# Encoder trunk on one core: x loaded once and transposed on TensorE, TensorE in the order of the source

## The chip, the core and the metric

The kernel runs on one core of a Trainium2 chip. A core has five engines, each with its own queue of instructions: TensorE (PE: products and transposes), VectorE (DVE), ScalarE (ACT), GpSimd (POOL) and SyncE (SP, which here only starts transfers), and 16 DMA engines. PE reads from SBUF and writes to PSUM, which holds eight banks here, four under the tag "g" and four under "y". The metric is the device time of one execution in microseconds; lower is better.

## The reference

Two layers over x of 256 positions by 1024 (float32). Cut to what matters:

```python
for l in range(2):
    h_res = h_res + 0.5 * swiglu(rmsnorm(h_res, ffn1_norm[l]), ffn1_w_gate[l], ffn1_w_up[l], ffn1_w_down[l])
    z = rmsnorm(h_res, mix_norm[l]) @ w_in[l]
    zq, zk, zv, zp, hq, hi, hff, hfb, hg = jnp.split(z, split_idx, axis=-1)
    y_att = dilated_attention(zq, zk, zv, q_norm[l], k_norm[l], biases)
    y_pool = pool_mixer(zp, pool_w[l], pool_scale[l])
    y_rec = hgrn2_bidirectional(hq, hi, hff, hfb, hg, lb_all[0, l], lb_all[1, l], hgrn_norm[l])
    h_res = h_res + jnp.concatenate([y_att, y_pool, y_rec], axis=-1) @ w_out[l]
    h_res = h_res + 0.5 * swiglu(rmsnorm(h_res, ffn2_norm[l]), ffn2_w_gate[l], ffn2_w_up[l], ffn2_w_down[l])
```

`swiglu` is `(silu(h @ w_gate) * (h @ w_up)) @ w_down` with a width of 2816. The recurrence (`hgrn2`) is a gated linear attention in both directions, with 4 heads of 64 each.

## The kernel before

x stays in SBUF as `self.x` (two tiles of 128 positions by 1024). The weights of all six stages (feed-forward, mixer, feed-forward, twice) stream through SBUF as 329 "halves" of 128x1024 float32 (512 KB), on SP's queue, through four buffers (`stage`). Each half is split into `whi` (rounded, by ACT, line 149) and `wlo` (the remainder, line 151, by DVE, or by POOL where the list `POOL_HALVES` names the half). Each product is made of three: hi by hi, hi by lo, lo by hi (lines 167 to 169 with 256 columns, lines 174 to 176 with 512). A half feeds 12 products of 512 columns or 24 of 256. The splits run `LOOK` = 4 halves ahead of the products, in five buffers.

*Feed-forward stage.* Eleven blocks of 256 of the width: `gate_up` makes gate and up of a block from four halves (48 products, `gu`), silu and product give `h`, `turn` transposes it (`hp`), and `down` adds the block of before to `ya`, from two halves. `ya` has four quarters, named by (dh, tt): 512 columns dh of the 128 positions tt.

*From stage to stage.* In the last `down` of a stage, each quarter is done after 6 products. Then `add` puts it on x (DVE, line 371), `squares` sums its squares for the norm (ACT, line 283), and `turn` transposes the four 128x128 blocks of the quarter (PE, `xps`, line 296); after both tt of a dh, `parts` splits the result into `xh` (ACT, line 274) and `xl` (DVE, line 275), the operands of the next stage. For quarter (1,1) the transposes are `pending`: `late_turn` runs them inside the next stage's first products. At the end of a mixer it is the same with `wo` in place of `ya`.

*Mixer.* After the gates, the steps of the string `ORDER` run: `c:n` makes the products of half n of the input projection (2 halves of hq, 4 each of q, k and zh, 2 of hg, 4 of v); `mm:m`, `up:m`, `put:m` are the levels of the recurrence (products `lev`, line 541, operands U and W updated by DVE in line 520, results put into A); `ns`, `nq`, `nk` scale and transpose q and k (`zq`, `tp`, line 660); `sc`, `tr`, `pv` are the attention; `rec` the product of the recurrence and `rnorm` its norm; `o` the output projection (`wo`).

*What sets the order.* SP issues in the order of the source. On the other engines a scheduler sets the order by its own estimates, within the dependencies, PE's queue too: a product can come ahead of transposes that stand before it in the source. Each engine then runs its queue in that order, and waits for what its next instruction needs.

*The start.* x comes in twice: in blocks already transposed (`x_t`, four transfers into the buffer of the later `bias`) between the two pieces of the first half on SP's queue, and as it is, on ACT's queue.

Of the kernel before, what the change touches and what calls it, by code (L numbers as in the profile page):

```python
# [16 lines left out]
P = 128  # L17
# [36 lines left out]
    ),  # L54
    (
# [8 lines left out]
T2 = 10  # L64
# [6 lines left out]
class Trunk:  # L71
    def __init__(self, ctx, tc, x_in, xt_in, wall, prm_in, rel_in, cst_in, cst2_in, msk_in, band_in, y_out):
# [18 lines left out]
        self.pending = None  # L91
# [11 lines left out]

        self.xt0 = self.bias[:, 0]
        self.cp.tile([P, 16], F32, name="pad0")
        xr = xt_in.rearrange("p (k t) -> p k t", k=KC)
# [3 lines left out]
        for j in range(4):  # L110
            if j < 2:
                q = slice(j * HALF // 2, (j + 1) * HALF // 2)
                nc.sync.dma_start(w0[:, q], wall[0][:, q])
            nc.sync.dma_start(self.xt0[:, 2 * j:2 * j + 2, :], xr[:, 2 * j:2 * j + 2, :])
        self.feed_dma(2)
        self.prm_in, self.cst_in = prm_in, cst_in
        self.ident = self.cst[:, K_ID:K_ID + P]
        nc.scalar.dma_start(self.ident, cst_in[:, K_ID:K_ID + P])
        nc.scalar.dma_start(self.x, x_in.rearrange("p (t d) -> p t d", t=2))
# [38 lines left out]
    def ahead(self, i):  # L158

        self.feed_dma(i + LOOK + 4)  # L160
        self.feed_split(i + LOOK)
# [21 lines left out]
    def late_turn(self):  # L183

        if self.pending is not None:
            self.pending()
            self.pending = None

    def gate_up(self, i0, gu, mid=None):

        for q in range(4):
            if q == 1:
                self.late_turn()
            if q == 2 and mid is not None:
                mid()
            self.ahead(i0 + q)
            wh, wl = self.half(i0 + q, 2)
            for tt in range(2):
                s = slice(tt * P, tt * P + P)
                for kk in range(2):  # L200
                    k = 2 * q + kk
                    self.mm3t(gu[tt], self.xh[:, k, s], self.xl[:, k, s], wh[:, kk, :], wl[:, kk, :],
                              start=(k == 0), stop=(k == KC - 1))
# [118 lines left out]
    def ffn(self, stage, post):  # L322
# [11 lines left out]
        for b in range(NB):  # L334
            if b == min(4, NB - 1) and stage == 0:
                self.setup(silu)
# [53 lines left out]
    def setup(self, after):  # L390
# [3 lines left out]
        mskf = self.mx.tile([P, 2 * len(LEVELS), 64], F32, tag="Kp", name="mskf", bufs=2)  # L394
        with self.tc.issue_after(after.ins):
            nc.scalar.dma_start(cst2, self.cst2_in)
            nc.scalar.dma_start(rel, self.rel_in)
            nc.scalar.dma_start(self.cst[:, K_BO:], self.cst_in[:, K_BO:])
            nc.scalar.dma_start(self.prm[:, C_PW:], self.prm_in[:, C_PW:])
            nc.scalar.dma_start(mskf, self.msk_in.rearrange("p (l c) -> p l c", c=64))  # L400
            nc.scalar.dma_start(self.band, self.band_in.rearrange("p (g s t) -> p g s t", g=4, s=2))
        nc.vector.tensor_copy(self.msk, mskf)
# [46 lines left out]
    def mixer(self, l):  # L449
# [106 lines left out]
        def lev_put(m):  # L556
# [20 lines left out]
            else:  # L577
                V["Ao"] = tl("Kp", [P, 8, P], bufs=2)
# [22 lines left out]
        def head_rs(sq, tag):  # L601
# [3 lines left out]
            hi, lo = self.split(sq)  # L605
# [176 lines left out]
        def out(nm):  # L782
# [14 lines left out]
            "rnorm": rec_norm, "o": out,  # L797
# [6 lines left out]
    def body(self):  # L804
        nc = self.nc
        self.new_xt()
        for j in range(4):
            if j < 2:
                self.split_part(0, j * HALF // 2, (j + 1) * HALF // 2)
            for k in (2 * j, 2 * j + 1):  # L810
                self.parts(0, k, self.xt0[:, k, :])
        self.n_split = 1
        self.feed_split(2)
        for dh in range(2):
            for tt in range(2):
                self.squares(0, dh, tt)
# [49 lines left out]
def _pack(inp):  # L866
# [40 lines left out]
    xt = np.ascontiguousarray(inp["x"][0].T.reshape(KC, P, T).transpose(1, 0, 2).reshape(P, KC * T))  # L907
    return x, xt, wall, prm
# [44 lines left out]
```

## Time and profile before

| | us |
|---|---|
| median of 3 runs (lowest to highest) | 1042.7 (1040.74 to 1046.78) |
| profiled execution, its own time | 1040.81 |
| its span, from first to last instruction | 1039.0 |
| PE busy | 1004.4 |
| DVE busy | 585.0 |
| ACT busy | 538.8 |
| POOL busy | 88.3 |
| mean granted clock of PE | 0.993 |

The span is what the trace shows; the execution's own time is 1.8 longer than it. A granted clock of 1.00 is 2.4 GHz and 0.50 is 1.2 GHz; the mean tells how much of the time PE ran at the higher level.

### The profile page before, as it was taken

How to read it: one execution, taken by the hardware profiler on the slowest of the kernel's cores; microseconds unless marked ns; L12 is line 12 of the kernel's file. 1: busy time of each engine (PE TensorE's matmuls, PEld its weight loads, DVE VectorE, ACT ScalarE, POOL GpSimd, SP SyncE). 2: the span in 40 equal slices, each digit the busy share in tenths (PEclk: the TensorE clock that was granted, in tenths of full speed). 3: DMA queues.
4: the chain of work that ended last, by engine and by line, in shares of the span. 5: the costliest groups of instructions: out<-in, count | busy, mean ns of one | idle time of the engine just before them, and what ended most of it. 6: DMA issues, size and time to landing. Idle time of an engine off the chain costs nothing.

```text
span 1039.0 us, 14421 instructions
## 1 busy us (share of the span) xinstructions
PE 1004.4 (97%) x5682; PEld 826.2 (80%) x5682; DVE 585.0 (56%) x776; ACT 538.8 (52%) x774; POOL 88.3 (8%) x43
## 2 busy tenths in 40 slices
PE   6999999998999999999999999999889999999998
PEld 4878888886867888888878888889768678888886
DVE  5655555669835555555565555554977155555553
ACT  7544444684865544444564444447648555444442
POOL 0000000140230000000000000004132400000000
PEclk9999999999999999999999999999989999999999
DMA  7769655553334555555555555554523346555551
GB/s 265 245 219 329 234 188 193 165 163 123 103 122 136 179 192 182 186 192 188 185 168 187 190 185 186 195 185 138 165 83 102 102 147 196 184 185 189 194 186 58
DMA packets 50420, 182.20 MB, mean 175 GB/s; under 512 B 5768, under 2 KB 6024, under 8 KB 49968
## 3 DMA queue, kind: packets, MB, share of 16 engines
q1 hardware_dynamic: 48528, 174.09, 51.6%
q0 software_dynamic: 720, 4.21, 1.1%
q10 hardware_dynamic: 1104, 2.99, 0.8%
q8 instruction: 44, 0.72, 0.3%
q14 instruction: 24, 0.20, 0.1%
HBM read 180.20 MB, written 3.16 MB: 176 GB/s over the span
## 4 chain that ended last, share of the span: by engine, by line
PE 87%; DVE 6%; ACT 3%; issue 3%; DMA 1%; POOL 0%; SPq 0%; ACTq 0%; DVEq 0%; POOLq 0%
PE gu L175 15%; PE gu L176 15%; PE gu L174 15%; PE ya L174 8%; PE ya L176 8%; PE ya L175 8%; PE hp L352 2%; PE wo L174 2%; PE wo L175 1%; PE wo L176 1%; ACT whi L149 1%; DVE wlo L151 1%; PE xps L296 1%; DMA bias<-x_t 1%; PE lev L541 1%
## 5 line engine op out<-in xcount | busy, mean ns | idle before, releaser
L149 ACT ACTIVATE whi<-stage 128x1024 fp32r<-128x1024 f32 (+1 forms) x329 | 347.1, 1056 | 395.3 <-PE gu L176 202.3
L151 DVE TENSOR_TENSOR wlo<-stage,whi 128x1024 fp32r<-128x1024 f32 (+1 forms) x294 | 360.7, 1229 | 337.5 <-ACT whi L149 337.4
L174 PE MATMUL gu<-whi,xh 128*128 128x512 f32 x704 | 275.7, 392 | 8.0 <-ACT xh L274 5.7
L175 PE MATMUL gu<-wlo,xh 128*128 128x512 f32 x704 | 274.9, 391 | 0.5 <-DVE wlo L151 0.5
L176 PE MATMUL gu<-whi,xl 128*128 128x512 f32 x704 | 274.7, 390 | 0.0
L174 PEld LDWEIGHTS gu<-whi,xh 128*128 128x128 f32 x704 | 132.5, 188 | 37.5 <-ACT xh L274 5.7
L175 PEld LDWEIGHTS gu<-wlo,xh 128*128 128x128 f32 x704 | 132.7, 189 | 28.7 <-DVE wlo L151 1.4
L176 PEld LDWEIGHTS gu<-whi,xl 128*128 128x128 f32 x704 | 132.6, 188 | 27.7
L174 PE MATMUL ya<-whi,hi 128*128 128x512 f32 x352 | 141.2, 401 | 0.0
L151 POOL TENSOR_TENSOR wlo<-stage,whi 128x1024 fp32r<-128x1024 f32 x35 | 85.0, 2437 | 654.5 <-ACT whi L149 639.2
L176 PE MATMUL ya<-whi,lo 128*128 128x512 f32 x352 | 137.8, 391 | 0.0
L175 PE MATMUL ya<-wlo,hi 128*128 128x512 f32 x352 | 137.4, 390 | 0.0
L176 PEld LDWEIGHTS ya<-whi,lo 128*128 128x128 f32 x352 | 66.1, 188 | 14.3
L175 PEld LDWEIGHTS ya<-wlo,hi 128*128 128x128 f32 x352 | 66.3, 188 | 12.4
L174 PEld LDWEIGHTS ya<-whi,hi 128*128 128x128 f32 x352 | 66.2, 188 | 12.3
L345 ACT ACTIVATE g<-gu,rc 128x256 f32<-128x256 f32 x88 | 41.5, 475 | 47.4 <-PE gu L176 47.4
L346 DVE SCALAR_TENSOR_TENSOR h<-gu,rc,g 128x256 f32<-128x256 f32 x88 | 42.0, 481 | 23.7 <-ACT g L345 23.7
L260 DVE TENSOR_TENSOR lo<-hp,hi 128x512 fp32r<-128x512 f32 x44 | 30.1, 684 | 2.8 <-ACT hi L259 2.8
L259 ACT ACTIVATE hi<-hp 128x512 fp32r<-128x512 f32 x44 | 25.6, 581 | 2.7 <-PE hp L352 2.7
L541 PE MATMUL lev<-U,W 64*64 64x64 f32 x384 | 15.6, 237 | 11.4 <-DVE W L520 11.4
L352 PEld LDWEIGHTS hp<-cst,h 128*128 128x128 f32 x176 | 21.8, 139 | 5.7
L352 PE MATMUL hp<-cst,h 128*128 128x128 f32 x176 | 26.3, 272 | 0.0
(224 smaller groups left out, 1035.8 us busy)
## 6 DMA issues: line engine op xcount, KB each, us to landing
stage<-w_all SPq DMA_DIRECT2D x327, 512.0 KB, 3.5
skew<-drow POOLq DMA_DIRECT2D x1, 2048.0 KB, 12.1
bias<-skew POOLq DMA_DIRECT2D x2, 1024.0 KB, 10.3
bias<-x_t SPq DMA_DIRECT2D x4, 256.0 KB, 7.9
x<-x ACTq DMA_DIRECT2D x1, 1024.0 KB, 8.4
band<-band ACTq DMA_DIRECT2D x1, 1024.0 KB, 8.0
y_t<-x SPq DMA_DIRECT2D x4, 256.0 KB, 2.2
stage<-w_all SPq DMA_DIRECT2D x2, 256.0 KB, 4.7
```

The lines of the kernel that those rows point to most:

```text
L149: nc.scalar.activation(hi[:, s], st[:, s], AF.Copy)
L151: eng.tensor_tensor(lo[:, s], st[:, s], hi[:, s].bitcast(F32), op=ALU.subtract)
L174: nc.tensor.matmul(out, lhsT=ah, rhs=wh, start=start, stop=False, skip_group_check=True)
L175: nc.tensor.matmul(out, lhsT=ah, rhs=wl, start=False, stop=False, skip_group_check=True)
L176: nc.tensor.matmul(out, lhsT=al, rhs=wh, start=False, stop=stop, skip_group_check=True)
L259: self.nc.scalar.activation(hi, src, AF.Copy)
L260: self.nc.vector.tensor_tensor(lo, src, hi.bitcast(F32), op=ALU.subtract)
L296: nc.tensor.transpose(self.xps[k // 2][:, j % 2, tt * P:tt * P + P], self.x[:, tt, k * P:k * P + P], self.ident)
L345: silu = nc.scalar.activation(g2[:, tt, :], gu[tt][:, 0:256], AF.Silu, scale=r)
L346: nc.vector.scalar_tensor_tensor(h[:, tt, :], gu[tt][:, 256:512], r, g2[:, tt, :], op0=ALU.mult, op1=ALU.mult)
L352: nc.tensor.transpose(hp[:, f, tt * P:tt * P + P], h[:, tt, f * P:f * P + P], self.ident)
L541: nc.tensor.matmul(ps[d][e * 64:e * 64 + 64, hb * 64:hb * 64 + 64], lhsT=a, rhs=c, start=(hb == 0), stop=(hb == 7), skip_group_check=True)
```

## The change

1. x is loaded once, in four pieces on SP's queue, the two pieces of the first weight half between the first two and the last two; the identity comes first on ACT's queue. The first stage's operands are made as in the later stages: 16 transposes on PE (`turn`), eight before the first products and eight, as `pending`, after the first 12. `x_t` and its buffer are gone.
2. Ahead of them stand 12 float32 products of ones, 128x128, whose result isn't used.
3. The splits start with no half ahead (`look` = 0), one ahead after the pending transposes, and 4 from the last quarter of the first block on, where the squares of x (`sums`) are issued too.
4. PE's queue is in the order of the source, as SP's is.
5. `ORDER` is another for both layers, `rnorm` is in two steps (`rn1` squares and their split, `rn2` the rest), and the pool of scratch tiles `t2` has 16 instead of 10.
6. The constants' transfers (`setup_loads`) are issued in block 3 and used (`setup`) in block 6; before, both in block 4.

The diff, cut to its core:

```diff
 ORDER = (
...
-        "c:0 ga c:1 gb c:2 uv c:3 c:4 c:5 mm:0 ns:q put:0 mm:1 up:2 c:6 put:1 mm:2 up:4 c:7 put:2 nq:0 c:8 mm:4 up:8 nq:1 put:4 "
...
+        "c:0 ga c:1 gb c:2 uv c:3 c:4 c:5 mm:0 ns:q put:0 c:6 mm:1 up:2 put:1 nq:0 c:7 c:8 mm:2 up:4 nq:1 c:9 put:2 mm:4 up:8 ns:k "
...
-T2 = 10
+T2 = 16
...
+        nc.scalar.dma_start(self.ident, cst_in[:, K_ID:K_ID + P])
         nc.scalar.dma_start(self.prm[:, 0:C_PW], prm_in[:, 0:C_PW])
         w0 = self.stage_t[0] = self.stg.tile([P, HALF], F32, tag="stage", name="stage")
         self.n_dma = 1
-        for j in range(4):
-            if j < 2:
-                q = slice(j * HALF // 2, (j + 1) * HALF // 2)
-                nc.sync.dma_start(w0[:, q], wall[0][:, q])
-            nc.sync.dma_start(self.xt0[:, 2 * j:2 * j + 2, :], xr[:, 2 * j:2 * j + 2, :])
+        for dh in range(2):
+            s = slice(dh * 512, dh * 512 + 512)
+            for tt in range(2):
+                nc.sync.dma_start(self.x[:, tt, s], xr[:, tt, s])
+            if dh == 0:
+                for j in range(2):
+                    q = slice(j * HALF // 2, (j + 1) * HALF // 2)
+                    nc.sync.dma_start(w0[:, q], wall[0][:, q])
...
-        self.feed_split(i + LOOK)
+        self.feed_split(i + self.look)
...
             self.pending()
             self.pending = None
+            self.look = min(self.look + 1, LOOK)
...
+            if q == 3 and self.then is not None:
+                self.then()
+                self.then, self.look = None, LOOK
...
-            if b == min(4, NB - 1) and stage == 0:
-                self.setup(silu)
+            if b == 3 and stage == 0:
+                self.setup_loads(silu)
+            if b == 6 and stage == 0:
+                self.setup()
...
+        def rec_squares():
+            sq = self.t2("sq")
+            nc.scalar.activation(sq, V["ops"], AF.Square)
+            V["osq"] = self.split(sq)
+
         def rec_norm():
             ops = V["ops"]
-            sq = self.t2("sq")
-            nc.scalar.activation(sq, ops, AF.Square)
-            rs = head_rs(sq, "rrs")
+            rs = head_rs(V["osq"], "rrs")
...
-        for j in range(4):
-            if j < 2:
-                self.split_part(0, j * HALF // 2, (j + 1) * HALF // 2)
-            for k in (2 * j, 2 * j + 1):
-                self.parts(0, k, self.xt0[:, k, :])
+
+        idle = self.pg.tile([P, 512], F32, tag="g", name="idle")
+        for _ in range(12):
+            self.nc.tensor.matmul(idle[:, 0:P], lhsT=self.ones, rhs=self.ones, start=True, stop=True)
+        for j in range(2):
+            self.split_part(0, j * HALF // 2, (j + 1) * HALF // 2)
         self.n_split = 1
-        self.feed_split(2)
-        for dh in range(2):
+        for tt in range(2):
+            self.turn(0, 0, tt)
+        self.feed_dma(5)
+
+        def second():
             for tt in range(2):
-                self.squares(0, dh, tt)
+                self.turn(0, 1, tt)
+
+        def sums():
+            for dh in range(2):
+                for tt in range(2):
+                    self.squares(0, dh, tt)
+
+        self.pending, self.then, self.look = second, sums, 0
...
-        ctx.enter_context(tc.manual_schedule(engines={mybir.EngineType.SP}))
+        ctx.enter_context(tc.manual_schedule(engines={mybir.EngineType.SP, mybir.EngineType.PE}))
```

Three places show how the order moves. The first is PE's queue at the end of stage 0. Before, its rows around the first two turns of x; the first row is the last product of the first three of quarter (0,1)'s six, and quarter (0,0) was done three products above it:

```order
L176 MATMUL ya<-whi,lo 128x512
L174 MATMUL ya<-whi,hi 128x512
L175 MATMUL ya<-wlo,hi 128x512
L176 MATMUL ya<-whi,lo 128x512
L174 MATMUL ya<-whi,hi 128x512
L175 MATMUL ya<-wlo,hi 128x512
L296 MATMUL xps<-cst,x 128x128 x4
L176 MATMUL ya<-whi,lo 128x512
L296 MATMUL xps<-cst,x 128x128 x4
L174 MATMUL ya<-whi,hi 128x512
```

Now, from the last product of quarter (0,0) on:

```order
L176 MATMUL ya<-whi,lo 128x512
L300 MATMUL xps<-cst,x 128x128 x4
L174 MATMUL ya<-whi,hi 128x512
L175 MATMUL ya<-wlo,hi 128x512
L176 MATMUL ya<-whi,lo 128x512
L174 MATMUL ya<-whi,hi 128x512
L175 MATMUL ya<-wlo,hi 128x512
L176 MATMUL ya<-whi,lo 128x512
L300 MATMUL xps<-cst,x 128x128 x4
L174 MATMUL ya<-whi,hi 128x512
```

The transposes of quarter (0,0) moved from eight products behind their quarter's last to straight behind it, and those of (0,1) from three behind to straight behind; those of (1,0), below the rows shown, moved in the same way.

The second is DVE's queue in layer 1's mixer, between the sums of squares of q (`hs`) and the scaling of q (`zq`). Before:

```order
L151 TENSOR_TENSOR wlo<-stage,whi 128x1024
L644 TENSOR_REDUCE hs<-sq 128x8
L520 TENSOR_TENSOR U<-U,dw 128x512
L520 TENSOR_TENSOR W<-W,dw 128x512
L651 TENSOR_TENSOR zq<-zq,hs 128x512 x2
L566 COPY_PREDICATED A<-msk,lev 128x512 x2
```

Now:

```order
L151 TENSOR_TENSOR wlo<-stage,whi 128x1024
L658 TENSOR_REDUCE hs<-sq 128x8
L151 TENSOR_TENSOR wlo<-stage,whi 128x1024
L665 TENSOR_TENSOR zq<-zq,hs 128x512 x2
L531 TENSOR_TENSOR U<-U,dw 128x512
L531 TENSOR_TENSOR W<-W,dw 128x512
```

The updates of U and W moved behind `zq`, and a weight split stands ahead of it.

The third is PE's queue there, around the first transposes of the scaled q (`tp`). Before:

```order
L176 MATMUL k<-whi,xl 128x512
L174 MATMUL k<-whi,xh 128x512
L175 MATMUL k<-wlo,xh 128x512
L176 MATMUL k<-whi,xl 128x512
L660 MATMUL tp<-cst,zq 128x128 x4
L174 MATMUL k<-whi,xh 128x512
```

Now:

```order
L552 MATMUL lev<-U,W 64x64 x2
L552 MATMUL lev<-W,U 64x64 x2
L552 MATMUL lev<-U,W 64x64 x2
L552 MATMUL lev<-W,U 64x64 x2
L674 MATMUL tp<-cst,zq 128x128 x4
L174 MATMUL k<-whi,xh 128x512
```

The transposes moved from within a later half of k to straight behind the first level product (`mm:1`), ahead of the second half of k.

## Rows read from the trace of the kernel before

**Rows 1.** the page's first section: busy us (share of the span), instructions; PE alone

```profile
PE 1004.4 (97%) x5682; PEld 826.2 (80%) x5682; DVE 585.0 (56%) x776; ACT 538.8 (52%) x774; POOL 88.3 (8%) x43
```

**Rows 2.** the waits of PE: engine line, releaser: us in total, times, longest

```profile
PE lev L541 <- DVE W L520: 11.4, 5, 4.5
...
PE wo L174 <- ACT hi L259: 4.5, 2, 2.2
PE xps L296 <- DVE x L371: 3.7, 5, 0.8
...
PE bps L405 <- DMA rel<-rel: 0.7, 1, 0.7
```

**Rows 3.** timeline of the start: start us, us, engine, line, what, [idle before <-releaser]

```profile
8.38 0.63 ACT L149 ACTIVATE whi<-stage 128x512 fp32r<-128x512 f32 x1 [2.28 <-DMA stage<-w_all]
...
11.24 0.63 PE L175 MATMUL gu<-wlo,xh 128*128 128x512 f32 x1
```

**Rows 4.** windows: us, busy us (instructions) by engine, PEclk, DMA share, GB/s

```profile
15.02:23.20 8.18, 8.18 (x35) 6.49 (x36) 4.74 (x6) 8.10 (x16) 0.00 (x0) 1.00 0.57 169
201.76:326.45 124.69, 117.64 (x1112) 97.37 (x1111) 81.47 (x156) 78.30 (x138) 36.31 (x15) 1.00 0.40 127
708.60:842.50 133.90, 123.45 (x1117) 102.42 (x1114) 79.87 (x146) 79.78 (x141) 43.91 (x18) 0.95 0.37 118
767.00:773.70 6.70, 5.21 (x72) 4.45 (x73) 5.73 (x8) 0.00 (x0) 0.79 (x1) 0.50 0.42 142
```

**Rows 5.** DMA rate over 0 to 30 us, 40 slices of 0.75 us

```profile
GB/s 0 0 118 307 265 314 385 366 396 393 333 249 380 440 407 426 421 426 421 311 66 93 268 371 284 284 104 5 0 87 328 300 169 213 393 355 399 415 361 377
```

**Rows 6.** timeline of the end of stage 0 and the start of the next

```profile
194.58 0.39 PE L176 MATMUL ya<-whi,lo 128*128 128x512 f32 x1
...
194.74 1.23 DVE L151 TENSOR_TENSOR wlo<-stage,whi 128x1024 fp32r<-128x1024 f32 x1 [1.35 <-ACT whi L149]
...
195.89 1.28 DVE L371 SCALAR_TENSOR_TENSOR x<-ya,x 128x512 f32<-128x512 f32 x2
...
196.37 1.06 ACT L149 ACTIVATE whi<-stage 128x1024 fp32r<-128x1024 f32 x1 [1.66 <-PE ya L176]
...
199.42 0.63 ACT L283 ACTIVATE sq<-x 128x512 f32<-128x512 f32 x1
...
200.05 0.82 ACT L274 ACTIVATE xh<-xps,prm 128x256 fp32r<-128x256 f32 x2
200.17 0.40 PE L176 MATMUL ya<-whi,lo 128*128 128x512 f32 x1
...
201.21 0.87 DVE L275 SCALAR_TENSOR_TENSOR xl<-xps,prm,xh 128x256 fp32r<-128x256 f32 x2
...
201.35 0.66 PE L296 MATMUL xps<-cst,x 128*128 128x128 f32 x4 [0.78 <-DVE x L371]
```

**Rows 7.** timeline of the end of stage 3: its first add

```profile
702.47 0.69 DVE L371 SCALAR_TENSOR_TENSOR x<-ya,x 128x512 f32<-128x512 f32 x1 [1.65 <-PE ya L176]
```

**Rows 8.** timeline of layer 0's mixer: two waits for W

```profile
238.22 0.27 PE L541 MATMUL lev<-U,W 64*64 64x64 f32 x2 [2.28 <-DVE W L520]
...
255.93 0.27 PE L541 MATMUL lev<-U,W 64*64 64x64 f32 x2 [1.85 <-DVE W L520]
```

**Rows 9.** timeline of layer 1's mixer, the q chain

```profile
735.45 1.22 DVE L509 TENSOR_TENSOR U<-q,dw 64x1024 f32<-64x1024 f32 x1
...
735.91 3.01 POOL L151 TENSOR_TENSOR wlo<-stage,whi 128x1024 fp32r<-128x1024 f32 x1 [8.87 <-ACT whi L149]
...
736.69 3.31 DVE L510 TENSOR_TENSOR W<-q,dw 64x1024 f32<-64x1024 f32 x1
...
744.77 0.68 DVE L644 TENSOR_REDUCE hs<-sq 128x8 f32<-128x512 f32 x1
...
745.95 1.04 ACT L149 ACTIVATE whi<-stage 128x1024 fp32r<-128x1024 f32 x1
...
746.56 1.29 DVE L651 TENSOR_TENSOR zq<-zq,hs 128x512 f32<-128x512 f32 x2
```

More of the change, by code (lines that the diff above doesn't have):

```diff
@@ L71, with __init__ @@
 class Trunk:
-    def __init__(self, ctx, tc, x_in, xt_in, wall, prm_in, rel_in, cst_in, cst2_in, msk_in, band_in, y_out):
+    def __init__(self, ctx, tc, x_in, wall, prm_in, rel_in, cst_in, cst2_in, msk_in, band_in, y_out):
         self.tc, self.nc = tc, tc.nc
@@ L90, in __init__ @@
         self.cur = 0
-        self.pending = None
+        self.pending = self.then = None
+        self.look = LOOK
         self.x = self.cp.tile([P, 2, D], F32, name="x")
@@ L101, in __init__ @@
         self.qgs = self.cp.tile([P, 8], F32, name="qgs")
-        self.xt0 = self.bias[:, 0]
-        self.cp.tile([P, 16], F32, name="pad0")
-        xr = xt_in.rearrange("p (k t) -> p k t", k=KC)
+        xr = x_in.rearrange("p (t d) -> p t d", t=2)
+        self.ident = self.cst[:, K_ID:K_ID + P]
+        nc.scalar.dma_start(self.ident, cst_in[:, K_ID:K_ID + P])
         nc.scalar.dma_start(self.prm[:, 0:C_PW], prm_in[:, 0:C_PW])
@@ L109, in __init__ @@
         self.n_dma = 1
-        for j in range(4):
-            if j < 2:
-                q = slice(j * HALF // 2, (j + 1) * HALF // 2)
-                nc.sync.dma_start(w0[:, q], wall[0][:, q])
-            nc.sync.dma_start(self.xt0[:, 2 * j:2 * j + 2, :], xr[:, 2 * j:2 * j + 2, :])
+        for dh in range(2):
[6 more added lines that the diff above has]
+                    nc.sync.dma_start(w0[:, q], wall[0][:, q])
         self.feed_dma(2)
         self.prm_in, self.cst_in = prm_in, cst_in
-        self.ident = self.cst[:, K_ID:K_ID + P]
-        nc.scalar.dma_start(self.ident, cst_in[:, K_ID:K_ID + P])
-        nc.scalar.dma_start(self.x, x_in.rearrange("p (t d) -> p t d", t=2))
         self.bones = self.cp.tile([P, P], F32R, name="bones")
@@ L387, in out_part, with setup_loads @@
         self.nc.sync.dma_start(yr[:, tt, s], self.x[:, tt, s])
-    def setup(self, after):
+    def setup_loads(self, after):
         nc = self.nc
@@ L393, in setup @@
         rel = self.mx.tile([32, 8], F32, tag="rel", name="rel")
-        mskf = self.mx.tile([P, 2 * len(LEVELS), 64], F32, tag="Kp", name="mskf", bufs=2)
+        mskf = self.mx.tile([P, 2 * len(LEVELS), 64], F32, tag="Kp", name="mskf")
         with self.tc.issue_after(after.ins):
@@ L401, in setup @@
             nc.scalar.dma_start(self.band, self.band_in.rearrange("p (g s t) -> p g s t", g=4, s=2))
+        self.later = cst2, rel, mskf
+    def setup(self):
+        nc = self.nc
+        cst2, rel, mskf = self.later
         nc.vector.tensor_copy(self.msk, mskf)
@@ L577, in lev_put @@
             else:
-                V["Ao"] = tl("Kp", [P, 8, P], bufs=2)
+                V["Ao"] = tl("Kp", [P, 8, P])
                 for d in range(2):
@@ L604, in head_rs @@
             f = lambda t: t.rearrange("p a t -> p (a t)")
-            hi, lo = self.split(sq)
+            hi, lo = sq
             nc.tensor.matmul(ps, lhsT=self.bones, rhs=f(hi), start=True, stop=False)
@@ L796, in mixer @@
             "nk": lambda j: qk_turn("k", j), "sc": att_scores, "tr": att_tr, "pv": att_pv, "rec": rec_mm,
-            "rnorm": rec_norm, "o": out,
+            "rn1": rec_squares, "rn2": rec_norm, "o": out,
         }
@@ L906, in _pack @@
     x = np.ascontiguousarray(inp["x"][0].reshape(2, P, D).transpose(1, 0, 2).reshape(P, 2 * D))
-    xt = np.ascontiguousarray(inp["x"][0].T.reshape(KC, P, T).transpose(1, 0, 2).reshape(P, KC * T))
-    return x, xt, wall, prm
+    return x, wall, prm
 def _constants():
@@ L941 @@
     inp = {k: np.asarray(v) for k, v in inputs.items()}
-    x, xt, wall, prm = _pack(inp)
+    x, wall, prm = _pack(inp)
     cst, cst2, msk, band = _constants()
-    arrays = dict(x=x, x_t=xt, w_all=wall, params=prm, rel=np.ascontiguousarray(inp["rel_bias"]), cst=cst, cst2=cst2, msk=msk, band=band)
+    arrays = dict(x=x, w_all=wall, params=prm, rel=np.ascontiguousarray(inp["rel_bias"]), cst=cst, cst2=cst2, msk=msk, band=band)
     nc = bacc.Bacc("TRN2", target_bir_lowering=False, num_devices=1)
```

14 rows, old and new, of the table ORDER are left out of this document.

## Prediction

> **What bounds the kernel now.** I read the page first: TensorE (PE) is busy 1004.4 us of a span of 1039.0 [rows 1], so only about 35 us are there to be gained or lost by order, and a change of this kind is worth what it does to PE's pauses. Next the waits of PE [rows 2]. They name where the pauses lie: five waits of the mixers' level products for W (11.4 us), two of the output projection for `hi` (4.5), one in each of the five stage transitions for the added x (3.7 in all), and one of 0.7 for a constant. A wait at a transition is short because PE has other products to run: the row shows one wait per transition, never three. Then the windows [rows 4]: the two mixers do the same products, but take 124.69 and 133.90 us for 117.64 and 123.45 us of busy PE, and in layer 1's stretch the mean granted clock is 0.95, with 0.50 (1.2 GHz, the lower level) from 767.0 to 773.7. The rest, the feed-forward blocks, runs without pauses and is changed only at its ends. So four places count: the start, the constants' wait, the transitions, the mixers.
>
> **The start.** Before, PE runs its first product at 5.75, pauses, works at slow products of 0.63 us [rows 3] and from 15.02 goes through without a pause: 35 products in 8.18 us, 0.234 each [rows 4]. The 14th product of block 0 starts at 15.02, so the 48th is done at about 23.0. After, the second piece of the first weight half stands behind 39 + 64 + 512 + 256 KB, in all 1.13 MB with itself. By the rate row [rows 5] the queues had moved 0.09, 0.32, 0.52, 0.75, 1.04 and 1.32 MB by the ends of slices 3 to 8, so 1.13 MB at about 5.5 us; pieces are seen later than that (before, that piece was used at 8.38 [rows 3], when the row gives 2.2 MB, of which 0.5 or more belong to later pieces). I take 6.7. ACT then has that piece (0.63 [rows 3]), four `xh` of 0.41 and two squares of 0.63 [rows 6] ahead of the second half's `whi`: 3.5, so it runs 10.2 to 11.3 (1.06 [rows 6]); DVE's `wlo` adds 1.23 [rows 6] and the handing over some 0.2: 12.7. Then 35 products of 0.234 are left: 20.9. Term: **-2.1**. Bounds: -3.5 if the pieces land at once, and +2.2 if the clock does not come up early: some 20 of these products at 0.43 instead of 0.234. The 0.43 is the spacing of the slow products before. The products of ones and the sixteen transposes of x themselves cost nothing: they lie ahead of the 6.7.
>
> The Trainium skill ("TensorE: Matmul & The Clock Gate", Part 1: The HAM clock gate) says that the throttled clock is the default and activity releases it. By that the products of ones should have the clock up for the first real products, which is the -2.1; nothing in the trace before shows PE working ahead of its data, so the other end stays in the range.
>
> **The constants.** PE waited 0.7 for `rel` [rows 2]; now the load is issued three blocks (some 50 us) ahead of its use. Term **-0.7**. The added weights of this are none: the same six transfers.
>
> **The transitions.** This is the largest term. The product order before lets the four transposes of a quarter of x run three to eight products after the add that they need (the order piece above), and PE was not stopped by the first three; only the fourth, which has nothing behind it, waits: the last product starts at 200.17, the transposes at 201.35 [rows 6], 1.18 for a spacing of 0.23, so 0.95 lost. After, PE keeps the order of the source: the transposes of quarters (0,0), (0,1) and (1,0) each stand straight behind the six products whose sum they need, with the whole rest of the stage queued behind them. Each of the three is then what the fourth was: 0.95. Only the fourth becomes free, since it now stands behind 12 or 24 products of the next stage (2.7 us or more).
>
> Two of the three are dearer. *First quarter:* its last product starts at 194.58, but DVE is in a `wlo` from 194.74 to 195.97 and adds at 195.89 [rows 6]; the transposes could run at 196.63, that is 2.05 behind the product, 1.83 lost. DVE's order keeps that `wlo` ahead of the add in four transitions; at the end of stage 3 it is on GpSimd and the add runs at once [rows 7]. *Third quarter:* in DVE's new order its add stands behind a pair of `xl`. Counted on from 196.63: transposes 0.41, five spacings of products to 198.17, add at 198.60 to 199.28, transposes at 199.35, next six products to 200.9, and the add could start at 201.3. But ACT has a `whi` (released by the same products, 198.6 to 199.65), the squares (0.63), two `xh` (0.41 each), and DVE two `xl` (0.87 the pair [rows 6]): it starts at 201.6, or at 201.85 where a `wlo` of 1.23 stands ahead of the `xl`. So 0.28 once and 0.54 four times.
>
> Sum: three waits of 0.95 in five transitions 14.25, the late `wlo` 4 x 0.88 = 3.5, the late third add 0.28 + 4 x 0.54 = 2.4, together 20.2; less the 4.75 that the five waits cost before: **+15.5**. Bounds: +9.5 if DVE is never behind, +24 if ACT's queue holds each third add for a further 1.7 (a `whi` and a square more).
>
> **Mixer of layer 0.** Idle PE is 124.69 - 117.64 = 7.05 [rows 4], of which the waits for W are 2.28 and 1.85 [rows 8] and one for `hi` 2.2 [rows 2]. The new order puts two halves of k (12 products each, 0.23 apart) ahead of the second level and one half between the later ones, and the squares of the recurrence get a half of products between them and their use. I take the 2.28 and 2.2 as gone, the 1.85 down to 0.5. New: `rec` needs a PSUM bank, of which v holds two and the last scores two; they come free when DVE has read them, behind the chain of `hg` (add-like 0.64, three ACT steps of 0.6, 0.64 again, two readings of some 0.4, from [rows 6] as nearest: 4.9), and only 12 products (2.7) stand between: 2.2. Small ones 0.5. After: 3.2. Term **-3.9**; bounds -6.4 (no new wait) and 0.
>
> **Mixer of layer 1.** It takes 133.90 where layer 0 is busy 117.64 [rows 4]: 16.3 of pauses and slow clock. After, the first turn of q (`nq:0`) stands right behind the first level product, a half earlier than its operands allow. PE is there 34.3 us into the stage (144 products of 256 columns at 0.12, five halves of 12 at 0.23, 3.2 for the turns and two level products), 742.9 on the clock of before. DVE's new order has `hs`, a `wlo`, then the two `zq`: `hs` runs 744.77 to 745.4, ACT its two small steps with a `whi` (1.04) between them, DVE the `wlo` (1.23), the `zq` pair (1.29) [rows 9]: ready at 749.3. A wait of **6.4**, the longest of the kernel, with everything of PE behind it. A wait of 4.5 [rows 2] went with 6.7 us at half the clock [rows 4], whose 5.21 busy us would have been 2.6 at the full one; I put 2.6 to this one too. Then `nk:0` 1.5 and small ones 0.7; the waits for W and `hi` go, since DVE gains what PE loses. After: 11.2. Term **-5.1**; bounds -14 and +3.
>
> **Sum.** -2.1 - 0.7 + 15.5 - 3.9 - 5.1 = +3.7 on the profiled execution's 1040.8: 1044.5. That execution is 1.9 below the median shown (1042.7), inside their spread of 6; I say **1045**.
>
> **Rivals.** *B, faster: the q chain is early.* DVE is late in layer 1 largely by one step: W at 736.69 took 3.31, beside a GpSimd split of 735.91 to 738.9, while its twin U took 1.22 [rows 9]. If the split falls elsewhere, W costs 1.2, `zq` comes 2.1 sooner, and with the `whi` and `wlo` of the chain (1.0 and 1.2) run before `hs` is there the wait is 2.1 instead of 6.4; no clock is lost (2.6), nor 1.5 at `nk:0`: 1044.5 - 4.3 - 2.6 - 1.5 = **1036**. Decides: a wait at `nq:0` under 2.5. Against: the rows of `hs` and `zq` stand behind that `wlo` in DVE's order.
> The Trainium skill ("GPSIMD Engine Reference", 1. Specifications) says that GpSimd's access to SBUF is shared with DVE and collides with DVE instructions of two SBUF inputs; the row of W agrees, 3.31 against 1.22, and by that rule the gain of B is there whenever the two part.
> *C, slower: ACT holds the third adds.* The bound above, 1.7 more in each transition: 1044.5 + 8.5 = **1053**. Decides: over 1 us at the third transposes beyond 0.95. For it: ACT's rows from 199.42 follow each other without a gap [rows 6].
> *D: the clock stays low at the start*: 1044.5 + 4.3 = **1049**. *E: the adds are never late*: 1044.5 - 5.9 = **1038.6**; against: the `wlo` at 194.74 stands in the row.
>
> **Chances.** Forecast 0.40 (own range 1040 to 1050), B 0.28, C 0.18, D 0.08, E 0.06. What a measurement tells from no change is about 0.5%, 5.2 us: faster is below 1037.5, slower above 1047.9. Faster: B 0.22, E 0.04, forecast 0.02: 0.28. Slower: C 0.16, D 0.05, forecast 0.11: 0.32. Same 0.40. The range leaves the lower edge of B and the upper of C out: 1030 to 1054.
>
> **What would show it.** Three waits of PE for x in each transition, 0.95 to 1.9, fifteen in all where there were five; no wait for `rel`; the first block's 48th product near 21; a wait of about 6 at the first `tp<-zq` in layer 1 and granted clock 0.50 behind it; one wait of `rec` in layer 0; few waits for W. The prediction is wrong if the transitions' transposes run without waits, or the mixers keep their waits for W.

## The result and the profile after

The changed kernel takes 1059.1 us in the median (1057.84 to 1060.26, 4 runs) against 1041.9 before (with a fourth run; 1040.74 to 1046.78); the ratio is 1.0156 (95% interval 1.012 to 1.0191). It is slower by 1.6%, above the upper end of the range (1054). The profiled execution has a span of 1058.5 (before 1039.0) and a mean granted clock of 0.988 (before 0.993). The two profiled executions lie near opposite ends of their kernels' runs (1060.3 and 1040.8), so the 19.5 between their spans is 2.3 more than the 17.2 between the medians.

First the page's line on PE, and the waits of PE (us in total, times, longest), which answer to [rows 1] and [rows 2]:

```profile
PE 1011.9 (96%) x5722; PEld 832.6 (79%) x5722; DVE 593.8 (56%) x776; ACT 539.2 (51%) x774; POOL 88.9 (8%) x43
```

```profile
PE xps L300 <- DVE x L377: 16.3, 15, 1.7
PE tp L674 <- DVE zq L665: 5.9, 2, 5.6
PE tp L674 <- DVE zk L665: 5.3, 2, 5.1
PE lev L552 <- DVE W L531: 4.1, 1, 4.1
PE lev L564 <- DVE W L531: 2.5, 2, 1.8
...
PE lev L560 <- DVE W L531: 1.5, 1, 1.5
PE sc L700 <- DVE Lk L678: 1.2, 1, 1.2
```

PE's busy time grew by 7.5 (the products of ones alone are 5.0, below); the span grew by 19.5, and most of that, 12.0, is idle time of PE. The waits for x at the transitions are now fifteen, 16.3 in all (before five, 3.7). The waits for `rel` and for `hi` ahead of the output projection are gone, and those for W went from 11.4 to 8.1 (lines 552, 560 and 564 together). In their place stand two of over 5 us for the scaled q and k (`zq`, `zk`), and smaller ones for `ops` (2.1) and `sc`.

The windows, as in [rows 4], cover the mixers from the first gate product to the last product of the first quarter of the output projection; the other two are stretches at the lower clock:

```profile
201.96:329.00 127.04, 119.58 (x1115) 99.90 (x1113) 84.47 (x156) 78.66 (x138) 36.94 (x15) 0.97 0.40 124
719.67:858.93 139.26, 123.50 (x1115) 101.46 (x1113) 85.72 (x145) 79.97 (x138) 43.98 (x18) 0.94 0.35 111
254.52:261.34 6.82, 5.71 (x75) 5.01 (x76) 6.82 (x11) 1.96 (x4) 0.00 (x0) 0.50 0.48 151
780.17:787.00 6.83, 5.55 (x15) 4.36 (x16) 2.92 (x5) 0.60 (x1) 0.00 (x0) 0.50 0.23 84
```

Layer 0's mixer takes 127.04 (before 124.69) and layer 1's 139.26 (before 133.90). In layer 0 PE now also falls to the clock of 0.50, from 254.5 to 261.3, which it didn't before (mean 1.00 then, 0.97 now). In layer 1 it has three stretches at 0.50, 17.1 us together, where it had three of 13.7 us together before.

The difference of the two spans, cut at the same products in both traces, is this. The fourth turn of a transition moved into the next stage (0.41, in the last stage 0.47 with what else moved); it is booked to the transitions:

| stretch | before | after | difference | forecast |
|---|---|---|---|---|
| to the last product of the first quarter of stage 0's last `down` (start, constants) | 194.58 | 192.32 | -2.3 | -2.8 |
| five transitions, with stages 2 and 3 around two of them | 7.18, 7.22, 374.93, 7.22 | 9.64, 9.82, 380.85, 9.83 | +13.6, with the moved turns +14.9 | +15.5 |
| mixer of layer 0 | 124.69 | 127.04 | +2.4, without the turn +1.9 | -3.9 |
| mixer of layer 1 | 133.90 | 139.26 | +5.4, without the turn +5.0 | -5.1 |
| sum | | | +19.5 | +3.7 |

The start, in PE's timeline (start, us, what, idle time before):

```profile
1.12 4.95 PE L824 MATMUL idle<-ones 128*128 128x128 f32 x24 [1.12 <-DVE ones L125]
...
11.64 0.40 PE L176 MATMUL gu<-whi,xl 128*128 128x512 f32 x1
...
21.28 0.39 PE L176 MATMUL gu<-whi,xl 128*128 128x512 f32 x1
```

The products of ones run from 1.12 to 6.1, and the first block's twelfth product starts at 11.64 with a length of 0.40, the length of the full clock; its 48th starts at 21.28.

The end of stage 0, which answers to [rows 6]:

```profile
192.32 0.39 PE L176 MATMUL ya<-whi,lo 128*128 128x512 f32 x1
192.48 1.23 DVE L151 TENSOR_TENSOR wlo<-stage,whi 128x1024 fp32r<-128x1024 f32 x1 [1.37 <-ACT whi L149]
...
194.36 0.66 PE L300 MATMUL xps<-cst,x 128*128 128x128 f32 x4 [1.65 <-DVE x L377]
...
196.01 0.40 PE L176 MATMUL ya<-whi,lo 128*128 128x512 f32 x1
...
197.19 0.66 PE L300 MATMUL xps<-cst,x 128*128 128x128 f32 x4 [0.78 <-DVE x L377]
...
198.84 0.40 PE L176 MATMUL ya<-whi,lo 128*128 128x512 f32 x1
...
200.09 0.66 PE L300 MATMUL xps<-cst,x 128*128 128x128 f32 x4 [0.85 <-DVE x L377]
```

Each of the three transposes stands right behind the product that it needs. The first waits from 192.32 to 194.36, 2.04, with DVE in the `wlo` of 192.48; the second 1.18, the third 1.25. Less a spacing of 0.23 these are 1.81, 0.95 and 1.02, against 1.83, 0.95 and 1.23 in the forecast.

Layer 0, where the eighth level waits (`mm:8`, answering to the second row of [rows 8]):

```profile
252.55 1.23 DVE L151 TENSOR_TENSOR wlo<-stage,whi 128x1024 fp32r<-128x1024 f32 x1 [1.00 <-ACT whi L149]
...
253.69 0.68 DVE L658 TENSOR_REDUCE hs<-sq 128x8 f32<-128x512 f32 x1
...
254.89 0.69 DVE L531 TENSOR_TENSOR W<-W,dw 128x512 f32<-128x512 f32 x1
...
255.63 0.37 PE L552 MATMUL lev<-U,W 64*64 64x64 f32 x2 [4.08 <-DVE W L531]
```

PE's last product before it starts at 251.16, and W is ready only at 255.6: in DVE's queue a weight split (`wlo`), which waits 1.00 for ACT's `whi`, and the second sums of squares of k (`hs`), whose squares ACT has ready only at 253.04, stand ahead of the updates of U and W.

Layer 1, around the q and the k chain, answering to [rows 9]:

```profile
759.62 0.47 PE L674 MATMUL tp<-cst,zq 128*128 128x128 f32 x1 [5.64 <-DVE zq L665]
...
774.88 2.37 POOL L151 TENSOR_TENSOR wlo<-stage,whi 128x1024 fp32r<-128x1024 f32 x1 [6.42 <-ACT whi L149]
...
775.96 1.84 DVE L531 TENSOR_TENSOR U<-U,dw 128x512 f32<-128x512 f32 x1
...
777.65 2.35 POOL L151 TENSOR_TENSOR wlo<-stage,whi 128x1024 fp32r<-128x1024 f32 x1 [0.40 <-ACT whi L149]
777.73 2.82 DVE L531 TENSOR_TENSOR W<-W,dw 128x512 f32<-128x512 f32 x1
...
781.29 0.45 PE L674 MATMUL tp<-cst,zk 128*128 128x128 f32 x1 [5.14 <-DVE zk L665]
```

The wait for `zq` is 5.64, close to the forecast 6.4. The wait for `zk` of 5.14 is the larger miss: U took 1.84 and W 2.82 where the same updates take 0.69 elsewhere, each beside a split on GpSimd. This pair was as long in the kernel before, beside the same two splits, and PE waited behind it for W instead:

```profile
762.67 2.37 POOL L151 TENSOR_TENSOR wlo<-stage,whi 128x1024 fp32r<-128x1024 f32 x1 [6.89 <-ACT whi L149]
763.75 1.85 DVE L520 TENSOR_TENSOR U<-U,dw 128x512 f32<-128x512 f32 x1
765.44 2.35 POOL L151 TENSOR_TENSOR wlo<-stage,whi 128x1024 fp32r<-128x1024 f32 x1 [0.40 <-ACT whi L149]
765.52 2.82 DVE L520 TENSOR_TENSOR W<-W,dw 128x512 f32<-128x512 f32 x1
...
768.49 0.37 PE L541 MATMUL lev<-U,W 64*64 64x64 f32 x2 [4.55 <-DVE W L520]
```

### The profile page after: what moved, and what is told of

It reads as the page before. It is cut to its first block, busy times and chain, and to the rows that moved or that the text cites. A ratio compares the mean times of both kernels' runs of the same rounds, so it can differ in the third digit from the quotient of the medians.

```text
span 1058.5 us, 14474 instructions
## 1 busy us (share of the span) xinstructions
PE 1011.9 (96%) x5722; PEld 832.6 (79%) x5722; DVE 593.8 (56%) x776; ACT 539.2 (51%) x774; POOL 88.9 (8%) x43
## 5 line engine op out<-in xcount | busy, mean ns | idle before, releaser
L300 PE MATMUL xps<-cst,x 128*128 128x128 f32 x96 | 14.9, 281 | 16.3 <-DVE x L377 16.3
L300 PEld LDWEIGHTS xps<-cst,x 128*128 128x128 f32 x96 | 10.5, 140 | 23.2 <-DVE x L377 22.7
```

Source lines behind the costliest of these rows:

```text
L300: nc.tensor.transpose(self.xps[k // 2][:, j % 2, tt * P:tt * P + P], self.x[:, tt, k * P:k * P + P], self.ident)
```

## The experiments

Four questions were put: whether it is PE's queue in the order of the source, or the new ORDER; whether the transitions and the mixers are separate; whether the mixers' waits are a matter of place or of DVE; and what the start's parts do. All ratios are to the kernel before, run on the same chip. "Before" had medians of 1041.5 to 1042.8 in these runs. The windows of a mixer are from one execution of each kernel, and the runs of one kernel lie some 1 to 9 us apart (before: 1036.8 to 1045.9 beside the first four experiments), so small differences between windows, of some 4 us or less, are not firm.

**PE scheduled again.**

```diff
-        ctx.enter_context(tc.manual_schedule(engines={mybir.EngineType.SP, mybir.EngineType.PE}))
+        ctx.enter_context(tc.manual_schedule(engines={mybir.EngineType.SP}))
```

> The changed kernel with one edit: PE's queue is ordered by the scheduler again, all else (start, ORDER, T2, constants) new. Theory S (PE stands still because the source puts steps ahead of their operands): the transitions have one wait of about 0.95 each again, which gives back 15 us, and the mixers' three long waits (4.2 in layer 0, 6.4 and 5.8 in layer 1) shrink by half or more: 1036 to 1041 us. Rival O (the new ORDER itself makes the mixers slow, whatever sets PE's queue): only the 15 come back and the mixers stay 8 us above those of before: 1044 us or more.

Measured: 1042.0 us, ratio 1.000 (0.9984 to 1.0016): 17 us less than the changed kernel, no different from before, and between the ranges of the two theories. The waits of PE, and the windows of the mixers:

```profile
PE tp L674 <- DVE zk L665: 4.7, 1, 4.7
PE tp L674 <- DVE zq L665: 4.3, 1, 4.3
...
PE xps L300 <- DVE x L377: 3.7, 5, 0.8
```

```profile
198.88:324.06 125.18, 118.36 (x1112) 98.88 (x1111) 83.22 (x156) 77.73 (x138) 36.13 (x15) 0.97 0.39 127
706.26:843.92 137.66, 124.03 (x1117) 101.75 (x1115) 86.17 (x146) 80.05 (x141) 44.02 (x18) 0.94 0.36 115
```

The transitions are back at one wait each. But the mixers kept nearly all: 125.18 and 137.66, and their long waits did not shrink by half, as theory S had it (4.7 and 4.3 here, 5.1 and 5.6 in the changed kernel). So the whole loss in the total goes with PE's queue in the order of the source, and still rival O may have a part: layer 1 with the new string is 3.8 slower than before (133.90) with a scheduled queue too, a difference that one execution of each doesn't make firm. The start (first gate product at 198.88, before 201.76) pays for it.

**The turns later, PE in the order of the source.**

```diff
-                self.turn(stage, dh, tt)
+                self.late.append([8 if (dh, tt) == (0, 0) else 5, lambda: self.turn(stage, dh, tt)])
```

`mm3t` counts these numbers down by one for each product, and runs the turn at zero.

> The changed kernel with the transposes of a quarter of x issued 8 products (first quarter) or 5 products (second and third) behind the products that they need, PE still in the order of the source. Theory S: nearly all of the three waits goes, 3.9 us a transition to under 0.8, in five transitions 14 to 16 us: 1043 to 1046 us, and the mixers as in the changed kernel. Rival: the adds and splits of DVE and ACT are late anyway, so PE waits for xh or xl at the start of the next stage instead: gain under 6 us, 1053 us or more.

Measured: 1047.3 us, ratio 1.004 (1.002 to 1.006): 11.8 less, a little short of the 14 to 16 expected. What is left shows at the first product of the next stage, which waits for `xl`:

```profile
197.45 0.48 PE L179 MATMUL ya<-whi,lo 128*128 128x512 f32 x1
199.10 0.39 PE L168 MATMUL ga<-xh,whi 128*128 128x256 f32 x1 [1.17 <-DVE xl L289]
```

The product at 197.45 and the next at 199.10 are 1.65 apart, 1.4 more than a spacing, where the kernel before lost 0.95.

**The strings of before, PE in the order of the source.** The two strings of ORDER are put back, with `rn1 rn2` for `rnorm`.

> The changed kernel with the ORDER strings of before (rnorm as rn1 rn2), PE in the order of the source. Theory S: the old strings put the level products right behind one half, so PE waits for W at mm:2 and mm:8 and for zq there: the mixers are no faster than with the new strings, 1057 to 1068 us. Rival O (the new strings are at fault): the mixers go back to the time of before, 7 to 8 us less: 1051 us or less.

Measured: 1059.6 us, ratio 1.0166 (1.013 to 1.0202): no change to the changed kernel's 1059.1. The mixers:

```profile
202.53:332.96 130.43, 120.67 (x1115) 100.11 (x1113) 83.33 (x156) 79.37 (x138) 36.62 (x15) 0.97 0.38 121
723.72:855.23 131.51, 119.78 (x1115) 99.87 (x1113) 81.19 (x145) 79.70 (x138) 43.46 (x18) 0.97 0.37 117
```

The total hides two opposite parts: with the old string layer 0 is 3.4 slower (130.43), layer 1 is 7.8 faster (131.51). The profiled execution of this run is the lowest of its runs (1056.6), that of the changed kernel the highest of its own (1060.3), so these parts do not add to the medians. In these executions the new string is better for layer 0 and worse for layer 1.

**The long waits' steps later in ORDER.** Of the strings, the part that differs (layer 0 first), lines joined:

```diff
-c:9 mm:4 up:8 ns:k put:4 c:10 mm:8 up:16 put:8 nk:0 c:11 nk:1 c:12 mm:16
+c:9 mm:4 up:8 ns:k put:4 c:10 c:11 mm:8 up:16 put:8 nk:0 c:12 nk:1 mm:16
...
-put:1 nq:0 c:7 c:8 mm:2 up:4 nq:1 c:9 put:2 mm:4 up:8 ns:k c:10 put:4 nk:0 c:11 mm:8 up:16 put:8 nk:1 c:12 sc:0 c:13 mm:16
+put:1 c:7 c:8 nq:0 mm:2 up:4 c:9 nq:1 put:2 mm:4 up:8 ns:k c:10 put:4 c:11 c:12 nk:0 mm:8 up:16 put:8 nk:1 c:13 sc:0 mm:16
```

> The changed kernel with the three steps that wait longest moved one or two halves later in ORDER (layer 0: mm:8 behind c:11; layer 1: nq:0 behind c:8, nk:0 and mm:8 behind c:12, sc:0 behind c:13). Theory S: the waits of 4.2, 6.4 and 5.8 fall to 3 or less together, and the slow clock behind them (some 5 us) goes: 13 to 18 us less, 1041 to 1046 us. Rival D (DVE is the limit in these stretches, its updates of W being slow beside GpSimd): the waits only move on to the next level product, gain under 6 us, 1053 us or more.

Measured: 1050.9 us, ratio 1.0083 (1.005 to 1.0116), 8 less. This lies between the ranges of the two theories, since each holds in one layer:

```profile
202.21:332.56 130.35, 121.84 (x1114) 101.38 (x1113) 87.93 (x156) 78.75 (x138) 36.64 (x15) 0.96 0.37 121
723.38:849.92 126.54, 119.24 (x1114) 99.10 (x1113) 85.50 (x145) 79.47 (x138) 45.57 (x18) 0.99 0.39 122
```

Layer 1 falls from 139.26 to 126.54, below the 133.90 of before. Layer 0 rises from 127.04 to 130.35: there only `mm:8` went later, with one half instead of two between it and the next level (`mm:16`). The wait moved on: `mm:8` waits 1.35 now, `mm:16` 2.62 and the first `sc` 1.35.

**Both together.** The later turns, and layer 1's new string; layer 0 keeps that of the changed kernel.

> The changed kernel with the later turns of the second experiment and, in layer 1 alone, the later steps of the fourth (layer 0 keeps the changed ORDER). If the two costs are separate, the gains add: 11.8 for the turns and 12.7 for layer 1's mixer (139.3 to 126.6 us): 1059.1 - 24.5 = 1034.6 us, range 1032 to 1037, below the kernel before. If they share a cause (DVE behind in both), less than 18 comes: 1041 us or more.

Measured: 1033.8 us, ratio 0.9913 (0.9898 to 0.9928). The two gains add (24.5 forecast, 25.3 measured), so the transitions and layer 1 were separate costs: the theory of one cause, with under 18, falls.

**Layer 0 spread in the same way.**

```diff
-c:10 mm:8 up:16 put:8 nk:0 c:11 nk:1 c:12 mm:16 up:32 put:16 sc:0 c:13 mm:32 up:64 put:32 sc:1
-c:14 mm:64 up:128 put:64 sc:2 tr:0 c:15 mm:128 put:128 join tr:1 sc:3 c:16 rec rn1 tr:2 band c:17 rn2 tr:3 tr:4 pool c:18 tr:5 tr:6
+c:10 c:11 mm:8 up:16 put:8 nk:0 c:12 nk:1 c:13 sc:0 mm:16 up:32 put:16 sc:1 c:14 mm:32 up:64 put:32 sc:2 tr:0
+c:15 mm:64 up:128 put:64 tr:1 sc:3 c:16 mm:128 put:128 join tr:2 band c:17 rec rn1 tr:3 tr:4 pool c:18 rn2 tr:5 tr:6
```

> The kernel of the fifth experiment with layer 0's ORDER spread over the later halves as in layer 1 (mm:8 behind c:11, mm:16 behind c:13, rec behind c:17). Theory S: the waits of 4.2 for mm:8 and 2.2 for rec and the slow clock behind them shrink, the mixer of layer 0 falls from 126.7 to 121 to 123 us: 4 to 6 us below the fifth. Rival: layer 0's DVE is the limit there and the wait moves on to the next level, as it did in the fourth experiment: within 2 us of the fifth.

Measured: 1029.6 us, ratio 0.9876 (0.9861 to 0.9891), 4.2 below the fifth.

```profile
199.74:321.37 121.63, 117.13 (x1113) 97.52 (x1114) 85.75 (x156) 78.45 (x138) 37.04 (x15) 1.00 0.39 130
```

Layer 0's mixer is at 121.63 with the full clock throughout, and its longest wait, for `mm:8`, is 1.38: the wait does not move on when the steps behind it go later too.

**The squares behind the turns.** The kernel of the fifth experiment, `squares` of a quarter called after its `turn` (those of the first quarter after the turn of the second).

> The kernel of the fifth experiment with the squares of a quarter issued behind its turn, so that ACT makes xh first. If ACT's queue (squares ahead of xh) is what leaves 1.4 us of waiting for xl at the start of each next stage, four or five of these waits shrink by 0.6 to 1.3: 3 to 5 us below the fifth. Rival: the sums then come late and the norm factors hold the first evacuation: no gain or slower.

Measured: 1034.3 us against 1033.8 of the fifth, the intervals overlap: no gain. The waits for `xl` at the next stage's start were the same 1.2. But the edit did not move what it was to move: ACT's queue is ordered by the scheduler, and its 774 instructions have the same order in both traces, with the squares of the third quarter still ahead of the second pair of `xh`:

```profile
197.51 0.63 ACT L297 ACTIVATE sq<-x 128x512 f32<-128x512 f32 x1
...
198.14 0.82 ACT L288 ACTIVATE xh<-xps,prm 128x256 fp32r<-128x256 f32 x2
```

So it says nothing on whether ACT's squares delay the `xl`; that stays open.

**Without the products of ones.**

```diff
-        idle = self.pg.tile([P, 512], F32, tag="g", name="idle")
-        for _ in range(12):
-            self.nc.tensor.matmul(idle[:, 0:P], lhsT=self.ones, rhs=self.ones, start=True, stop=True)
```

> The changed kernel without the products of ones. If they are what has the clock up for the first products of the first stage, the first block's products run at 0.43 instead of 0.23 for a while and its 48th product moves from 21.3 to 23 to 25.5 us in the profile, the rest being as it was. If the transposes or the first products would bring the clock up as early, it stays within 0.5 of 21.3. Rival forecast of mine (case D) is that the clock came up no earlier with them: then nothing moves.

A single run took 1060.4 us, as long as the profiled execution of the changed kernel (1060.3), so the total shows no gain of theirs. PE's timeline of the first block, its first, twelfth and 48th product:

```profile
7.92 0.80 PE L174 MATMUL gu<-whi,xh 128*128 128x512 f32 x1 [1.41 <-ACT xh L278]
...
12.83 0.63 PE L176 MATMUL gu<-whi,xl 128*128 128x512 f32 x1
...
22.77 0.39 PE L176 MATMUL gu<-whi,xl 128*128 128x512 f32 x1
```

The twelve products take 4.91 from the first to the last, 0.63 each, where they took 3.36, most of them at 0.39 or 0.40, with the ones ahead of them, and the 48th starts at 22.77 instead of 21.28: 1.5 later, which is a little less than the 1.7 to 4.2 expected. So of the start's gain some 1.5 are theirs, in this pair of executions. The length of 0.63 is that of the lower clock: products of the same size have it from 783.0 on in the changed kernel, in the stretch with a granted clock of 0.50 shown above (in this run the record of the granted clock begins only behind these twelve, so it does not show their level). The Trainium skill ("TensorE: Matmul & The Clock Gate", Part 1: The HAM clock gate) has the lower clock as the default that activity lifts; this pair of runs agrees, 0.63 against 0.39 for the same product.

**Three splits of layer 1 on DVE instead of GpSimd.**

```diff
-(2, 5, 6, 7, 8, 12, 16, 18, 19, 20, 21,
+(2, 5, 6, 7, 8, 16, 20, 21,
```

> The changed kernel with three of layer 1's weight splits (halves 12, 18 and 19 of POOL_HALVES[1]) on DVE instead of GpSimd: the ones that run beside DVE's first W (3.30 us) and beside the U and W ahead of zk (1.84 and 2.82). If the GpSimd split beside them is what stretches these updates, they fall to 1.2, 0.7 and 0.7, and the wait for zk falls from 5.8 to 2 to 4 (DVE has two splits of 1.23 more there); the time stays within 4 us of the changed kernel's 1059, since DVE pays for the splits. If the updates stay long, GpSimd is not their cause.

Measured: 1052.6 us, ratio 1.0096 (1.008 to 1.0113), 6.5 less than the changed kernel. In DVE's timeline the first W, and U and W ahead of `zk`:

```profile
748.45 1.22 DVE L521 TENSOR_TENSOR W<-q,dw 64x1024 f32<-64x1024 f32 x1
...
776.56 0.68 DVE L531 TENSOR_TENSOR U<-U,dw 128x512 f32<-128x512 f32 x1
...
777.16 0.69 DVE L531 TENSOR_TENSOR W<-W,dw 128x512 f32<-128x512 f32 x1
```

```profile
720.45:852.29 131.84, 120.17 (x1115) 99.11 (x1113) 83.57 (x148) 79.98 (x138) 36.33 (x15) 0.97 0.35 117
```

W fell from 3.30 to 1.22, U from 1.84 to 0.68, W from 2.82 to 0.69, as expected; the longest wait for `zk` is 2.5 instead of 5.1, and layer 1's mixer fell from 139.26 to 131.84, although DVE has three splits of 1.23 more. The gain was larger than the 4 us expected at most. So some 7.4 of layer 1's time hung on DVE being held beside GpSimd. That does not add to the 12.7 of the fourth experiment: both shorten the same waits, one by making the steps' operands earlier, the other by asking for them later. And the kernel before had the same hold, so the new order did not bring it.

**The later strings with a scheduled PE.** The strings of the sixth experiment, PE's queue left to the scheduler.

> The sixth experiment's ORDER strings with PE's queue left to the scheduler and without the later turns written out. If the order of the steps in ORDER is what makes the mixers fast, and the order of the source itself gives nothing, this is as fast as the sixth: 1027 to 1032 us. If PE in the order of the source with the right strings is better than the scheduler, this is 4 us or more above the sixth (over 1033).

Measured: 1028.0 us, ratio 0.9863 (0.9845 to 0.9881), 1.6 below the sixth.

```profile
198.99:320.19 121.20, 116.78 (x1113) 97.07 (x1111) 85.71 (x156) 78.08 (x138) 37.01 (x15) 1.00 0.38 130
702.41:828.02 125.61, 117.83 (x1116) 97.96 (x1115) 85.27 (x146) 79.60 (x141) 44.65 (x18) 1.00 0.38 126
```

The strings make the mixers fast, 121.20 and 125.61, whether PE runs in the order of the source or not. The order of the source by itself gives nothing; where the source has a step early, it costs. Whether it costs anything with late steps, the 1.6 doesn't tell, since the two intervals overlap.

**The same, with fewer splits on GpSimd.** The tenth and the sixth, each with halves 12, 16 and 20 of layer 0 and 12, 18 and 19 of layer 1 split on DVE.

> The tenth experiment's kernel (PE scheduled, later strings) with six weight splits that run beside DVE's updates on DVE instead of GpSimd: halves 12, 16 and 20 in layer 0, 12, 18 and 19 in layer 1. If the slowing of DVE beside GpSimd still holds PE up in these strings, W falls from 3.4 to 1.2 in both layers and the waits for zq and zk shrink: 2 to 5 us below the tenth (1023 to 1026 us). If the later strings already hide it, within 2 us of 1028; if DVE becomes the limit by the six splits (7.4 us more work), slower.

> The sixth experiment's kernel (PE in the order of the source, later turns, later strings) with the same six splits on DVE. Same theory: 2 to 5 us below the sixth (1025 to 1028 us); with the eleventh it shows again whether the order of the source costs anything once steps stand late enough (then this is 1 to 2 us above the eleventh, as the sixth was above the tenth).

Measured: 1021.7 us, ratio 0.9808 (0.9776 to 0.9839), with PE scheduled, and 1023.4, ratio 0.9823 (0.9786 to 0.9861), in the order of the source: 6 below each one's partner, more than the 2 to 5 expected. The eleventh is 1.9% faster than the kernel before. Its list of PE's waits has none for `zq` or `zk` (the tenth: 2.5 and 1.4), and the longest sum in it is again the five waits for x, 3.7. In this pair, run on one chip, the order of the source is 1.7 slower, and the two kernels' runs do not overlap (at most 1021.9, at least 1022.7).

## Why the prediction was wrong, point by point

**The start** held: -2.3 measured against -2.8 for start and constants. The 48th product started at 21.28 and was done at 21.67, against 20.9 for its end in the forecast. The twelfth and 48th product ran at the full clock, so case D did not come, and the eighth experiment shows that a part of it, 1.5 of its 4.3, would have come without the products of ones. One reading was wrong and cost little: eight of the sixteen transposes do not lie ahead of the data but among the products, at 11.87.

**The transitions** held, the largest term: +14.9 against +15.5, and the first two waits one by one. Only the third was shorter in all five (1.02 against 1.23 in the first transition, 1.17 or 1.18 against 1.49 in the others), so its late add was put too dear by 1.5 in all; 0.9 of that was made up elsewhere, which is not traced. Case C (the third add held by another 1.7) and case E (no add late) fell.

**The mixers failed, and they alone make the miss of 15.8** (+19.5 against +3.7; the misses of the other two terms, +0.5 and -0.6, cancel). Layer 0 came out 5.8 above the forecast and layer 1 10.0 above it.

In layer 0 the step "I take the 2.28 and 2.2 as gone, the 1.85 down to 0.5" is the wrong one: the first two are gone and the new wait of `rec` came as put (2.07 against 2.2), but `mm:8` waits 4.08 instead of 0.5. I put PE's time against the place of `mm:8`, but not DVE's queue, in which a split and the `hs` of k, both held by ACT, stand ahead of the updates. Idle time is 7.5 instead of 3.2. The clock of 0.50, which I had put at nothing in layer 0, came too, with 6.8 us: PE's busy time is 1.5 above the 117.64, without the moved turn.

In layer 1 the step "Then `nk:0` 1.5 and small ones 0.7; the waits for W and `hi` go, since DVE gains what PE loses" is wrong. The wait for `zq` was right (5.9 against 6.4), yet DVE gained nothing by it: it had the updates of U and W behind `zq`, and then took 4.66 instead of 1.4 for the pair ahead of `zk`, beside two splits on GpSimd. So `zk` was waited for 5.3, and two later levels and `sc` for 1.8, 1.5 and 1.2 (lines 564, 560 and 700), 9.8 together where I had 2.2. Idle time is 15.8 instead of 8.6, and PE's busy time is 2.9 above the 117.64 and 2.6 that I had, without the moved turn: a second long stretch of the clock of 0.50 (780.17 to 787.00) came with the wait for `zk`.

The trace before showed what this step missed. Its longest wait for W, 4.55 at 768.49, stood behind the same pair, held in the same way (1.85 and 2.82). I took that wait as gone because its place in PE's queue changed; what made it, DVE held beside two splits, stayed, and the next step that needs DVE waited 5.14 instead. Of the slow clock before I read one stretch; the mean of 0.95 in its row stands for twice as much, and the trace has two more, of 3.4 each.

**What the runs put in its place.** The loss to before goes with PE's order (the first experiment: 17 us, all of it), two thirds of it in the transitions (the second: 11.8). In the mixers the waits are a matter of place (the fourth and sixth experiments: layer 1 to 126.5, layer 0 to 121.6), and in layer 1 also of DVE held beside GpSimd (the ninth: 7.4, which overlaps with the gain of place). Rival B had that mechanism for the first W alone, and had it end if the split fell elsewhere; the first W stayed as long as it was (3.30 against 3.31), and the pair of U and W was in no theory.

**Chances.** The forecast of no change had 0.40, slower 0.32, and half of the slower one (0.16) was tied to the transitions' third add. No rival had the mixers slower than before, though both had a bound near zero for it (0 and +3); the measured +1.9 and +5.0 lie outside both.

## What to carry to other kernels

Before an engine's queue is pinned to the order of the source, look at where the scheduler had put each step whose operand comes from another engine: every such step that stands right behind its producer in the source becomes a wait with the whole queue behind it (here three in each transition, 0.94 to 1.86 each). When a wait is to go because its step moves, look first at what makes the operand late and whether that moves too. Price a step that is moved by the queue of the engine that makes its operand, instruction by instruction and with what that engine shares, and not by the consumer's time alone. When a wait goes later, move the chain behind it too, or it moves on to the next link.

## What the hardware showed that was not expected

A two-operand update on DVE that starts while a GpSimd split runs ends only some time after the split has ended, nearly its own length later: U started at 775.96, the split ran from 774.88 to 777.25, and U ended at 777.80, 0.55 later; W started at 777.73, the split ended at 780.00, W at 780.55, again 0.55 later (its usual length is 0.68). All five updates of U and W (128x512) of the changed kernel's layer 1 that start beside a split in this way end 0.55 behind it, and the first W (64x1024, usually 1.22) 1.08 behind its split. A sum with one operand, the `hs` at 775.36, ran beside the same split in its usual 0.69. In the ninth experiment, without these splits, the U and W ahead of `zk` are at 0.68 and 0.69. The Trainium skill ("GPSIMD Engine Reference", 1. Specifications) has GpSimd's access to SBUF shared with DVE, with contention for instructions of two SBUF inputs; this agrees, and the rows show that the price was nearly the whole rest of the split.

The clock came into layer 0 too. Before, its mixer had waits of 2.28 and 1.85 and a mean granted clock of 1.00 [rows 4, 8]; after, it fell to 0.50 within the one wait of 4.08 and stayed there from 254.5 to 261.3. PE was busy for 5.7 us of that stretch, and its busy time in the mixer is 1.5 higher than before, without the moved turn.
